# Odd dilated scores: four 64x64 quarters replaced by two 64x128 halves with zero queries

## The chip, the cores and the metric

The kernel runs on one core of a Trainium2 chip. The metric is device time in microseconds (us) for one launch. Before the change it is 736.02 us, the median of three runs from 735.62 to 736.18. One more execution was recorded by the hardware profiler; it took 735.57 us, and its trace spans 733.8 us from the first to the last instruction. The TensorE matmul unit is called PE in the profile and its weight load PEld; VectorE is DVE, ScalarE is ACT, GpSimd is POOL, and SP issues most DMAs.

## The reference, cut to what matters

The network has 256 tokens of width 1024 and two layers. Layer 0 (even) mixes tokens with neighbourhood and latent attention, layer 1 (odd) with dilated sliding windows; each is followed by a squared-ReLU MLP. Only the odd layer's attention is touched. It has three groups of 16 heads, each head 64 wide, with its own queries, keys and values after rotary embedding:

```python
DIL_PAIRS = ((128, 1), (512, 4), (2048, 16))   # (window, dilation)
...
offsets = [jnp.arange(-(w // 2), w // 2 + 1, d) for (w, d) in DIL_PAIRS]
...
kpos = qpos[:, None] + offsets[gi][None, :]
valid = (kpos >= 0) & (kpos < s)
sc = jnp.einsum('bqhd,bqjhd->bhqj', q_blk[:, :, gi], k_sel) * scale
```

Group 0 lets a query see every key within 64 positions. Group 1 lets it see keys whose distance is a multiple of 4, group 2 a multiple of 16; with 256 tokens their windows cut off next to nothing. The three groups are combined by their softmax denominators, which is one softmax over all the scores of a query together.

## The kernel before, in words

**Token order.** The host permutes the tokens so that positions 64c to 64c+63 hold the 64 tokens with the same remainder c modulo 4. A query of group 1 or 2 sees keys of its own class of 64 only. The 256 tokens are two token tiles of 128, and each tile holds two classes. Masks take away what a group does not see.

**Precision.** The projections are computed from f32 numbers split into a high and a low part (lines 178 and 179), with two or three matmuls for each product (lines 182 to 184, 188 and 189); their operands have the type fp32r. The scores of groups 1 and 2 and the products with the values are plain f32 matmuls; each shows in the trace as two weight loads and two matmuls. PE transposes (line 936) show as one of each.

**The odd layer's order.** The heads are taken two at a time, which gives eight units. For a unit, `qk_steps` (line 859) runs twelve projection steps: three weight tiles b (queries and keys of group 0, queries of groups 1 and 2, keys of groups 1 and 2), two halves f and two halves of the contraction. After the last step of a b, `rope` (line 879) applies the rotary embedding by four small DMAs on SP and three operations on DVE. The last DVE operation writes `q12` or `k12` (line 890). Both are tiles of 128 partitions, two heads of 64 rows each, by two groups by 256 tokens. Each is allocated anew for every unit from two rotating buffers (`unit_tiles`, line 816).

After the sixth step of the next unit's projections, a burst is placed in PE's order by hand (`beside` and `burst`, lines 976 to 991): at some units the products with the values (`mix`, lines 953 and 958), then the transposes of the previous unit's first token tile (`turn`, line 936), the group 0 scores (`two_heads`, line 203), the transposes of the second tile, and the scores of groups 1 and 2 (line 914). There are eight bursts; the first has no transposes and the last comes at step 14 of unit 7. After a burst PE goes on with the projections (lines 188 and 189, or 182 to 184 for the values).

**The lines around the change.** For each token tile i, group g, class c and head j, line 914 multiplies 64 rows (the head's width) by 64 queries as the stationary operand and 64 keys as the moving one. The output has 64 partitions and 64 columns. The four combinations of c and j sit on the four quarters of PE's 128x128 array. A bank of PSUM for each (i, j) holds 256 columns of group 0 scores and 2 x 64 columns of the others. DVE then adds the mask and takes the minimum over 384 columns (line 920), ACT takes the exponential (line 922), and DVE and ACT divide by the sum (lines 923 and 924).

**What sets the order.** Every engine runs its own instructions in order. A planner orders them from the program's order and its priorities, and it places semaphores and buffer addresses; `soon()` and `NORM_PRIO` raise the priority of what empties PSUM. A phase's buffers take the addresses of the phase before and wait for them tile by tile (line 1011). POOL runs a few small operations; in the odd layer that is one reciprocal square root (line 258). SP issues the odd layer's tables (line 813) and then its weights, in order.

Of the kernel before, what the change touches and what calls it, by code (L numbers as in the profile page):

```python
# [16 lines left out]
F32 = mybir.dt.float32  # L17
F32R = mybir.dt.float32r
AF = mybir.ActivationFunctionType
ALU = mybir.AluOpType  # L20
# [3 lines left out]
P = 128  # L24
D = 1024
KT = D // P
T = 256
NT = T // P
# [18 lines left out]
def trunk(ctx, tc, a, out):  # L47
    nc = tc.nc
# [8 lines left out]
    def scratch(shape, name):  # L57

        n = int(np.prod(shape))
        v = work.tile([P, 512], F32, tag="scratch", name=name, bufs=12)[:, :n]  # L60
        if len(shape) == 2:
            v = v.rearrange("p (a b) -> p a b", b=shape[1])
        return v
# [8 lines left out]
    def quarter_pair(name):  # L72
        return pair_tile(act, KT // 2, name, 2, "quarter")

    def halves(z):

        return (z[:, 0, :], z[:, 1, :]) if len(z.shape) == 3 else (z[:, :, 0, :], z[:, :, 1, :])

    def bank(tag):
        return ps.tile([P, 512], F32, tag=tag, name=tag)  # L80
# [88 lines left out]
    def weight():  # L169

        j = state["used"]
        prefetch(j + 1, j + 1)
        prefetch(j + LOAD_AHEAD, j + SPLIT_AHEAD)
        state["used"] = j + 1
        return parts.pop(j)[1:]

    def split(hi, lo, src, eng=None):
        a = nc.scalar.copy(hi, src).ins  # L178
        return a, (eng or nc.vector).tensor_tensor(lo, src, hi.bitcast(F32), op=ALU.subtract).ins  # L179
# [6 lines left out]
    def mm2(o, sh, sl, m, first, last):  # L186

        both = lambda: nc.tensor.matmul(o, sh, m.rearrange("p v n -> p (v n)"), start=first, stop=last)  # L188
        low = lambda: nc.tensor.matmul(o[:, 0:T], sl, m[:, 0, :], start=False, stop=False)  # L189
        for step in (low, both) if last else (both, low):  # L190
            step()

    def joined(dst, o):

        nc.scalar.copy(dst, o[:, T:2 * T])  # L195
        nc.vector.tensor_tensor(dst, dst, o[:, 0:T], op=ALU.add)  # L196

    def two_heads(o, qk, ts):

        for n, (a, b) in enumerate(((0, 0), (0, 1), (1, 0))):  # L200
            for j in range(2):
                pb = slice(64 * j, 64 * j + 64)
                nc.tensor.matmul(o[j], qk[pb, 0, a, ts], qk[pb, 1, b, :], start=n == 0, stop=n == 2)  # L203
# [10 lines left out]
    def soon():  # L214

        return tc.high_priority(DRAIN_PRIO)

    def tok(t):
        return slice(t * P, (t + 1) * P)
# [587 lines left out]
    def odd(op, xT, s):  # L807
# [5 lines left out]
            nc.sync.dma_start(dst, a[nm])  # L813
        mixed = [quarter_pair("oa"), quarter_pair("ob")]

        def unit_tiles(u):
            d = {}
            for n, shape, dt in (("q0", [P, 2, 2, T], F32R), ("q12", [P, 2, T], F32), ("k12", [P, 2, T], F32)):
                d[n] = op.tile(shape, dt, tag=n, name=n, bufs=2)
            return d  # L820

        values = {}
# [36 lines left out]
        def qk_steps(d):  # L859


            hold = {}

            def gemm(b, f, half):
                if f == 0 and half == 0:
                    hold["w"], hold["s"] = weight(), scratch([2, T], "qk")
                if half == 0:
                    hold["p"] = bank("acc")
                (wh, wl), s, pq = hold["w"], hold["s"], hold["p"]
                for k in range(4 * half, 4 * half + 4):  # L870
                    ws = slice((f * KT + k) * P, (f * KT + k + 1) * P)
                    mm2(pq, wh[:, ws], wl[:, ws], xT[:, k], k == 0, k == KT - 1)
                if half == 1:
                    with soon():
                        joined(s[:, f], pq)
                if f == 1 and half == 1:
                    rope(b, s)

            def rope(b, s):
                sw, r1 = scratch([2, T], "sw"), scratch([2, T], "r1")  # L880
                for r in range(0, P, 64):
                    nc.sync.dma_start(sw[r:r + 32], s[r + 32:r + 64])
                    nc.sync.dma_start(sw[r + 32:r + 64], s[r:r + 32])
                nc.vector.tensor_tensor(r1, s, cosT.unsqueeze(1).broadcast_to([P, 2, T]), op=ALU.mult)
                nc.vector.tensor_tensor(sw, sw, sinT.unsqueeze(1).broadcast_to([P, 2, T]), op=ALU.mult)
                if b == 0:
                    nc.vector.tensor_tensor(r1, r1, sw, op=ALU.add)
                    split(*halves(d["q0"]), r1)
                else:
                    nc.vector.tensor_tensor(d[("q12", "k12")[b - 1]], r1, sw, op=ALU.add)  # L890

            return [lambda v=(b, f, h): gemm(*v) for b in range(3) for f in range(2) for h in range(2)]

# [9 lines left out]
        def scores(u, d, between):  # L903

            ss = {(i, j): bank("w") for i in range(NT) for j in range(2)}
            for i in range(NT):
                two_heads([ss[i, j][:, 0:T] for j in range(2)], d["q0"], tok(i))
            between()
            for i in range(NT):
                for g in range(2):  # L910
                    for c in range(2):
                        for j in range(2):
                            pb, own = slice(64 * j, 64 * j + 64), slice(i * P + 64 * c, i * P + 64 * c + 64)
                            nc.tensor.matmul(ss[i, j][64 * c:64 * c + 64, T + 64 * g:T + 64 * g + 64], d["q12"][pb, g, own],
                                             d["k12"][pb, g, own], start=True, stop=True)
            for i in range(NT):
                for j in range(2):
                    sn, pp = scratch([384], "sn"), op.tile([P, 384], F32, tag="pp", name="pp", bufs=4)
                    mn, z, rz = (work.tile([P, 1], F32, tag=v, name=v, bufs=4) for v in ("dmn", "dz", "drz"))
                    nc.vector.tensor_tensor_reduce(out=sn, in0=ss[i, j][:, 0:384], in1=mask[:, i, :], op0=ALU.add, op1=ALU.min,  # L920
                                                   scale=-(HD ** -0.5), scalar=3e38, accum_out=mn)
                    nc.scalar.activation(pp, sn, AF.Exp, bias=mn, scale=-1.0, accum_out=z)
                    nc.vector.reciprocal(rz, z)
                    nc.scalar.activation(pp, pp, AF.Copy, scale=rz)
                    probs[u, i, j] = pp
# [16 lines left out]
        def mix(u0, out_tag):  # L942
# [17 lines left out]
            with soon():  # L960
                split(*halves(mixed[u0 // 4][:, u0 % 4:u0 % 4 + 2]), pvo.rearrange("p (u n) -> p u n", u=2))

        units = [unit_tiles(0)]
        d = units[0]
        products, v_out = value_steps(0)
# [17 lines left out]
        def burst(u):  # L983

            def step():
                if u > 1 and u % 2:
                    mix(u - 3, "acc")
                if u > 0:
                    turn(u - 1, 0, "acc")
                scores(u, units[u], lambda: turn(u - 1, 1, "acc") if u > 0 else None)  # L990
            return step

        for u in range(1, 8):
            units.append(unit_tiles(u))
            placed = {5: burst(u - 1)}
            if u == 7:
                placed[13] = burst(7)
            beside(qk_steps(units[u]) + all_values(u), placed)
# [17 lines left out]
    accs, last, scale = phase("mlp0", mlp_between, xT, s)  # L1016
    xT, s = hand_over_tokens(accs, last, 2, scale)
    accs, last = phase("odd", odd, xT, s)
    xT, s = hand_over(accs, last, 3)
    phase("mlp1", finish, xT, s)  # L1020
# [98 lines left out]
```

## Time and profile before

| what | value |
|---|---|
| time, median of three runs | 736.02 us (735.62 to 736.18) |
| time of the profiled execution | 735.57 us |
| its span | 733.8 us |
| PE matmul busy | 723.0 us, 99% |
| PE weight load busy | 626.1 us, 85% |
| DVE busy | 536.9 us, 73% |
| ACT busy | 452.4 us, 62% |
| POOL busy | 5.7 us, 1% |
| line 914: matmul records | 256, 218 ns each (median) |
| line 914: weight loads | 256, 135 ns each (median) |

The busy time of PE is made of matmuls that overlap: their ends are modelled, and the next one starts before the record of the last is over. So a busy PE is no proof that PE is at its peak, and the distance from one start to the next says more than a duration. Shapes are written rows*columns of the array in use, then the moving operand: "64*128 64x256" is 64 rows by 128 stationary columns with 256 moving columns. In the timeline, neighbouring records of one kind are merged into a row with their count; the first number is the start, the second the length from the first start to the last end.

### The profile page before, as it was taken

The page shows a single profiled execution, that of the slowest core. Times are in us where ns is not written, and L with a number is a line of the kernel's source. Part 1 is how long each engine was busy: PE and PEld are TensorE (multiplying, and loading weights), DVE is VectorE, ACT ScalarE, POOL GpSimd, SP SyncE. Part 2 cuts the span into 40 slices and gives each one's busy share as a digit, 9 for nine tenths or more (in the row PEclk, how much of TensorE's full clock was granted, in tenths as well). Part 3 has the DMA queues.
Part 4 walks back from the last instruction along what each step waited for, and adds up shares of the span by engine and source line. Part 5 has one row for each costly group of instructions (what it writes and reads, how often), then busy time and mean ns, then how long its engine had stood idle before and what let it go on. Part 6 is the DMA issues. An engine that isn't in the chain of part 4 may idle for free.

```text
span 733.8 us, 12891 instructions
## 1 busy us (share of the span) xinstructions
PE 723.0 (99%) x5004; PEld 626.1 (85%) x5004; DVE 536.9 (73%) x1078; ACT 452.4 (62%) x1002; POOL 5.7 (1%) x16
## 2 busy tenths in 40 slices
PE   8999999999999999999999999999999999999996
PEld 5899989888888888888888888888998888888885
DVE  6799859756656656889778889778759666665664
ACT  7687857445445446856777667767857445544541
POOL 0100000000000000000000000000000000000000
PEclk9999999999999999999999999999999999999999
DMA  8864423565565554566755665466345556456501
GB/s 288 340 226 153 146 96 125 210 209 180 186 206 182 186 204 158 198 215 209 245 167 178 205 202 202 154 221 200 130 169 206 196 175 225 174 172 209 181 14 57
DMA packets 26989, 135.72 MB, mean 185 GB/s; under 512 B 4400, under 2 KB 7216, under 8 KB 12336
## 3 DMA queue, kind: packets, MB, share of 16 engines
q1 hardware_dynamic: 26640, 134.69, 53.2%
q8 instruction: 39, 0.64, 0.3%
q10 hardware_dynamic: 288, 0.21, 0.1%
q14 instruction: 22, 0.18, 0.1%
HBM read 127.55 MB, written 1.05 MB: 175 GB/s over the span
## 4 chain that ended last, share of the span: by engine, by line
PE 86%; DVE 4%; DMA 3%; ACT 3%; issue 2%; SPq 1%; POOL 0%; POOLq 0%
PE w L188 16%; PE acc L182 13%; PE acc L183 13%; PE acc L184 13%; PE acc L188 12%; PE w L189 8%; PE acc L189 6%; DVE wlo L179 2%; DMA raw<-in_w_c 1%; DMA raw<-in_w_qk 1%; ACT pp L734 1%; DMA bias<-in_rpb 1%; PE w L203 1%; PE acc L936 1%; PE acc L953 1%
## 5 line engine op out<-in xcount | busy, mean ns | idle before, releaser
L179 DVE TENSOR_TENSOR wlo<-raw,whi 128x512 fp32r<-128x512 f32 (+2 forms) x472 | 301.9, 681 | 70.5 <-ACT whi L178 68.8
L178 ACT CAST whi<-raw 128x512 fp32r<-128x512 f32 (+2 forms) x472 | 262.8, 617 | 86.1 <-issue 70.4
L188 PE MATMUL w<-xT,whi 128*128 128x512 f32 x512 | 178.2, 393 | 0.0
L188 PE MATMUL acc<-xT,whi 128*128 128x512 f32 x384 | 133.1, 395 | 0.0
L189 PE MATMUL w<-xT,wlo 128*128 128x256 f32 x512 | 132.8, 280 | 0.0
L188 PEld LDWEIGHTS w<-xT,whi 128*128 128x128 f32 x512 | 93.6, 188 | 17.3
L189 PEld LDWEIGHTS w<-xT,wlo 128*128 128x128 f32 x512 | 96.4, 188 | 5.3
L189 PE MATMUL acc<-xT,wlo 128*128 128x256 f32 x384 | 99.6, 280 | 0.0
L182 PE MATMUL acc<-whi,h 128*128 128x512 f32 x250 | 98.1, 392 | 0.0
L183 PE MATMUL acc<-wlo,h 128*128 128x512 f32 x250 | 97.5, 390 | 0.0
L184 PE MATMUL acc<-whi,h 128*128 128x512 f32 x250 | 97.4, 390 | 0.0
L188 PEld LDWEIGHTS acc<-xT,whi 128*128 128x128 f32 x384 | 69.6, 188 | 12.8
L195 ACT COPY up<-w 128x256 f32<-128x256 f32 x64 | 23.9, 373 | 87.3 <-PE w L188 87.2
L189 PEld LDWEIGHTS acc<-xT,wlo 128*128 128x128 f32 x384 | 72.2, 188 | 3.7
L196 DVE TENSOR_TENSOR up<-up,w 128x256 f32<-128x256 f32 x64 | 26.8, 419 | 61.4 <-ACT up L195 61.4
L184 PEld LDWEIGHTS acc<-whi,h 128*128 128x128 f32 x250 | 46.9, 188 | 9.8
L183 PEld LDWEIGHTS acc<-wlo,h 128*128 128x128 f32 x250 | 47.0, 188 | 9.6
L182 PEld LDWEIGHTS acc<-whi,h 128*128 128x128 f32 x250 | 47.0, 188 | 8.8
L183 PE MATMUL acc<-wlo,xT 128*128 128x512 f32 (+1 forms) x128 | 50.4, 394 | 0.8 <-DVE wlo L179 0.8
L182 PE MATMUL acc<-whi,xT 128*128 128x512 f32 (+1 forms) x128 | 50.5, 394 | 0.5 <-ACT whi L178 0.5
L184 PE MATMUL acc<-whi,xT 128*128 128x512 f32 (+1 forms) x128 | 50.0, 391 | 0.0
L855 ACT ACTIVATE v<-acc,rstd 64x128 f32<-64x128 f32 x64 | 22.8, 362 | 19.7 <-PE acc L184 14.0
(203 smaller groups left out, 981.7 us busy)
## 6 DMA issues: line engine op xcount, KB each, us to landing
raw<-in_w SPq DMA_DIRECT2D x64, 1024.0 KB, 4.8
raw<-in_w_oqk SPq DMA_DIRECT2D x24, 1024.0 KB, 5.0
raw<-in_w_ov SPq DMA_DIRECT2D x12, 1024.0 KB, 5.3
sw<-qk SPq DMA_DIRECT2D x96, 64.0 KB, 3.1
raw<-in_w_qk SPq DMA_DIRECT2D x4, 1024.0 KB, 11.1
raw<-in_w_oe SPq DMA_DIRECT2D x4, 1024.0 KB, 5.0
raw<-in_w_oo SPq DMA_DIRECT2D x4, 1024.0 KB, 5.9
bias<-in_rpb SPq DMA_DIRECT2D x8, 256.0 KB, 4.3
```

Of the source, the lines that this page charges most:

```text
L178: a = nc.scalar.copy(hi, src).ins
L179: return a, (eng or nc.vector).tensor_tensor(lo, src, hi.bitcast(F32), op=ALU.subtract).ins
L182: nc.tensor.matmul(o, sh, mh, start=first, stop=False)
L183: nc.tensor.matmul(o, sh, ml, start=False, stop=False)
L184: nc.tensor.matmul(o, sl, mh, start=False, stop=last)
L188: both = lambda: nc.tensor.matmul(o, sh, m.rearrange("p v n -> p (v n)"), start=first, stop=last)
L189: low = lambda: nc.tensor.matmul(o[:, 0:T], sl, m[:, 0, :], start=False, stop=False)
L195: nc.scalar.copy(dst, o[:, T:2 * T])
L196: nc.vector.tensor_tensor(dst, dst, o[:, 0:T], op=ALU.add)
L203: nc.tensor.matmul(o[j], qk[pb, 0, a, ts], qk[pb, 1, b, :], start=n == 0, stop=n == 2)
L734: nc.scalar.activation(pp[:, j], sn[:, j], AF.Exp, bias=mn[:, j:j + 1], scale=-1.0, accum_out=z[:, j:j + 1])
L855: nc.scalar.activation(v12[64 * g - 64:64 * g, 2 * i + c, :], pq[rows, cs], AF.Copy, scale=ri[rows])
```

## The change

The tile for the queries of groups 1 and 2 is no longer one of two rotating buffers. Two tiles named `spread0` and `spread1` are made once at the start of the odd phase, and the units use them in turn. Each holds, for every group and token tile, three blocks of 64 columns: the queries of class 0, zeros, the queries of class 1. POOL writes the zeros once. The DVE operation at the end of the rotary embedding writes its 512 columns into blocks 0 and 2 instead of into a dense tile.

The scores then take 128 stationary columns: blocks 0 and 1 for class 0 (its queries, then zeros), blocks 1 and 2 for class 1 (zeros, then its queries). The output has all 128 partitions of the bank. The matmul of class 0 starts the accumulation and that of class 1 adds to it in the same 64 columns, so each query's row gets its own class's scores plus zeros. The number of matmuls stays the same (16 in a burst, 128 in all), and so do the moving columns.

```diff
+        spread = [op.tile([P, 2 * NT, 3, 64], F32, name=f"spread{i}") for i in range(2)]
+        for z in spread:
+            nc.gpsimd.memset(z[:, :, 1, :], 0.0)
+
         def unit_tiles(u):
             d = {}
-            for n, shape, dt in (("q0", [P, 2, 2, T], F32R), ("q12", [P, 2, T], F32), ("k12", [P, 2, T], F32)):
+            for n, shape, dt in (("q0", [P, 2, 2, T], F32R), ("k12", [P, 2, T], F32)):
                 d[n] = op.tile(shape, dt, tag=n, name=n, bufs=2)
+            d["q12"] = spread[u % 2]
             return d
...
+                elif b == 1:
+                    own = lambda z: z.rearrange("p g (t c n) -> p (g t) c n", t=NT, c=2)
+                    nc.vector.tensor_tensor(d["q12"][:, :, 0:3:2, :], own(r1), own(sw), op=ALU.add)
                 else:
-                    nc.vector.tensor_tensor(d[("q12", "k12")[b - 1]], r1, sw, op=ALU.add)
+                    nc.vector.tensor_tensor(d["k12"], r1, sw, op=ALU.add)
...
                     for c in range(2):
                         for j in range(2):
                             pb, own = slice(64 * j, 64 * j + 64), slice(i * P + 64 * c, i * P + 64 * c + 64)
-                            nc.tensor.matmul(ss[i, j][64 * c:64 * c + 64, T + 64 * g:T + 64 * g + 64], d["q12"][pb, g, own],
-                                             d["k12"][pb, g, own], start=True, stop=True)
+                            nc.tensor.matmul(ss[i, j][:, T + 64 * g:T + 64 * g + 64], d["q12"][pb, 2 * g + i, c:c + 2, :],
+                                             d["k12"][pb, g, own], start=c == 0, stop=c == 1)
```

## The prediction

> **What bounds the kernel now.** I read the page's share of engines first, then the busy time in the stretches of the odd layer, then PE's timeline around a burst, then the weight loads grouped by shape.
>
> ```profile
> PE 723.0 (99%) x5004; PEld 626.1 (85%) x5004; DVE 536.9 (73%) x1078; ACT 452.4 (62%) x1002; POOL 5.7 (1%) x16
> ...
> 306.00:330.00 24.00, 24.00 (x142) 20.95 (x142) 20.68 (x41) 14.66 (x35) 0.00 (x0) 1.00 0.64 216
> ...
> sum 224.00, PE 224.00 PEld 193.97 DVE 185.47 ACT 163.64 POOL 0.00; mean PE 28.00 PEld 24.25 DVE 23.18 ACT 20.45 POOL 0.00
> ```
>
> The stretch rows give the length, then the busy time of PE, PEld, DVE, ACT and POOL, the granted clock (1.00) and DMA figures; the last row sums eight stretches from 306 to 530 us, which hold all eight bursts. PE is busy in 224.00 of 224.00 us there. DVE has 38.5 us to spare, ACT 60. So a microsecond added to PE's work in this stage finds no pause in which to disappear. One burst, the second, and the first of all:
>
> ```profile
> 359.68 0.41 PE L936 MATMUL acc<-ident,pp 64*128 64x64 f32 x8
> 359.90 0.96 PE L203 MATMUL w<-q 64*128 64x256 f32 x12
> 360.70 0.53 PE L936 MATMUL acc<-ident,pp 64*128 64x64 f32 x12
> 361.16 0.69 PE L914 MATMUL w<-k,q 64*64 64x64 f32 x32
> 361.78 0.50 PE L188 MATMUL acc<-xT,whi 128*128 128x512 f32 x1
> ...
> 329.87 0.97 PE L203 MATMUL w<-q 64*128 64x256 f32 x12
> 330.78 0.69 PE L914 MATMUL w<-k,q 64*64 64x64 f32 x32
> 331.40 0.50 PE L188 MATMUL acc<-xT,whi 128*128 128x512 f32 x1
> ```
>
> ```profile
> L914 PE MATMUL w<-k,q x256: 218/218/267, 330.8 to 516.0; 64*64 64x64 f32 x128
> L936 PE MATMUL acc<-ident,pp x168: 213/222/273, 359.5 to 515.4; 64*128 64x64 f32 x168
> L203 PE MATMUL w<-q x96: 275/280/383, 329.9 to 514.9; 64*128 64x256 f32 x96
> ```
>
> (Durations are shortest, median, longest in ns.) A merged row's last start is its start plus its length less one duration. In the second burst the last transpose (line 936) starts at 360.70 + 0.53 - 0.222 = 361.01, the quarters (line 914) start at 361.16, and the projection goes on at 361.78. **The stretch that the change touches is 361.78 - 361.01 = 0.77 us.** It holds a pause of 0.15 us from a 64*128 shape to the quarters, 32 records in eight steps of four (last start 361.16 + 0.69 - 0.218 = 361.63, so 0.47 us, 0.06 a step), and a pause of 0.15 us to the full array. In the first burst it begins at the last group 0 score, 329.87 + 0.97 - 0.28 = 330.56, and lasts 0.84 us. That the eight are alike is seen in their busy time:
>
> ```profile
> 330.50:331.80 1.30, 0.69 (x32) 0.56 (x32) 1.00 0.56 126
> ...
> sum 10.45, PE 5.56 PEld 4.46; mean PE 0.69 PEld 0.56
> ```
>
> **The change part by part.** *The matmuls.* Their number and moving columns stay. They use 64 rows and all 128 columns, so two run side by side (the two heads) where four did: 32 records become 16 steps of two instead of eight of four. What a step costs hangs on the weight load, which doubles to 128 columns. The loads, grouped by shape (busy us, mean ns of one):
>
> ```profile
> L203 PEld LDWEIGHTS w<-q 64*128 64x128 f32 x96 | 6.2, 187 | 0.3 <-ACT whi L178 0.3
> L936 PEld LDWEIGHTS acc<-ident,pp 64*128 64x128 f32 x168 | 6.7, 138 | 1.2 <-ACT whi L178 0.7 <-issue 0.2
> L914 PEld LDWEIGHTS w<-k,q 64*64 64x64 f32 x256 | 4.5, 134 | 0.6
> L958 PEld LDWEIGHTS acc<-pts,v 128*64 128x64 f32 x96 | 4.4, 138 | 0.0
> L250 PEld LDWEIGHTS w<-mean,squares 128*128 128x128 f32 x16 | 2.4, 190 | 0.3
> L319 PEld LDWEIGHTS w<-ident,down 128*128 128x128 f32 x16 | 1.8, 140 | 0.8 <-ACT down L317 0.6
> ```
>
> Loads of 64 columns take 134 to 138 ns, loads of 128 columns 187 to 190, whether 64 rows (line 203) or 128 (line 250, a plain f32 matmul like ours). The two rows with 128 columns at 138 and 140 are transposes, whose moving operand is the identity. The difference of about 53 ns for 64 columns makes about 107 ns for 128, with a fixed part that overlaps. The distance from load to load confirms it:
>
> ```profile
> 303.97 0.30 PEld L250 LDWEIGHTS w<-mean,squares 128*128 128x128 f32 x2
> ...
> 359.87 0.55 PEld L203 LDWEIGHTS w<-q 64*128 64x128 f32 x8
> ...
> 359.98 0.67 PEld L203 LDWEIGHTS w<-q 64*128 64x128 f32 x10
> ```
>
> Line 250 moves one column (its matmul is 128x1), so its load alone paces it: 0.30 - 0.19 = 0.11 us apart. Line 203 has our shape and loads for two heads side by side: the ten loads from its second pair on are five pairs, (0.67 - 0.187) / 4 = 0.120 us apart, and there 256 columns are moved as well. The new matmul moves far less: the quarters' step of 0.06 us holds their whole move. So the load sets the step, between 0.11 and 0.120. I take 0.117, near line 203, whose shape and pairing it shares.
>
> Pauses. The transposes already use 64*128, so the 0.15 us before the quarters goes. Line 203 after the transposes shows what stands there: the last of the eight transposes starts at 359.68 + 0.41 - 0.222 = 359.87, and line 203's first loads start at 359.87 too, its second pair at 359.98. So I count 16 steps from the last transpose's start to the last score's, the last one from its load to its matmul. The pause after stays: from the wide shape to the full array it is 0.16 us, by the last transposes, 530.71 + 0.72 - 0.222 = 531.21 to 531.37:
>
> ```profile
> 530.71 0.72 PE L936 MATMUL w<-ident,pp 64*128 64x64 f32 x18
> 531.37 0.39 PE L182 MATMUL acc<-oa,whi 128*128 128x256 f32 x1
> ```
>
> So a stretch becomes 16 x 0.117 + 0.15 = 2.02 us. That is 2.02 - 0.77 = 1.25 more in seven bursts and 2.02 - 0.84 = 1.18 in the first: 7 x 1.25 + 1.18 = **9.9 us**. By 0.11 a step it is 7 x 1.14 + 1.07 = 9.1, by 0.120 it is 7 x 1.30 + 1.23 = 10.3.
>
> A rule stands against the slow load. The Trainium skill (TensorEngine Tiling (Array Packing), Restrictions) says that column tiling disables the fast weight load; the quarters are column tiling and the new shape is not. But TensorE: Matmul & The Clock Gate (Weight-path perf modes) of the same skill gives the fast load only to 128 weights that are not FP32. By the first rule alone the new loads would be as quick as the transposes', by the second as slow as line 203's; the load rows side with the second for everything that is not a transpose.
>
> *The DVE write into blocks 0 and 2, and the zeros.* The eight writes keep 512 elements a partition:
>
> ```profile
> L890 DVE TENSOR_TENSOR q<-r,sw x8: 679/682/686, 326.5 to 508.5; 128x512 f32<-128x512 f32 x8
> ...
> 304.63 0.70 POOL L258 TENSOR_TENSOR rstd<-ms,mhalf 128x2 f32<-128x2 f32 x1 [269.04 <-DVE ms L252]
> ...
> L105 POOL MEMSET mean<- 128x128 f32 x1 | 0.2, 206 | 0.0
> ```
>
> No row shows a write in 64-column pieces. If it took half as long again, eight times 0.34 = 2.7 us would go onto DVE, which has 38.5 spare; the bounds for the path are 0 and, with that cover gone, 2.7; I take 0. The two memsets of 256 columns are at most 0.4 us each by the 0.2 of 128 columns; POOL waits 269 us before its only odd operation, so the cover is that pause. Behind them in POOL's queue stands that operation alone. They must come before 304.63; the tiles whose addresses they take are the MLP's, whose matmuls end ahead of the odd layer's first projection. *Buffer waits.* The next write to a spread tile waits for the scores two units before, as the rotating buffers did. The scores of a burst end 1.25 us later; behind line 914 on PE stand the projections, already counted, and DVE's mask step (line 920) starts that much later with the next unit's projections ahead of the transposes that need its result. *Addresses.* The odd phase needs 2 KB a partition more, which shifts later tiles. The queue on which that could matter is SP's:
>
> ```profile
> SPq L813 <- PE acc L184: 7.9, 1, 7.9
> ```
>
> SP already stands 7.9 us at an odd table until the MLP's matmuls free its place, with the odd weights behind it. PE does not pause for that today. Bounds: nothing, to about 3 us if the shift made weights late; I take nothing.
>
> **Sum.** Span 733.8 + 9.9 = 743.7; the profiled execution 735.57 + 9.9 = 745.5. That execution is 0.45 below the median of the runs, which gives 745.9. I forecast 745.7.
>
> **Rivals.** *Quick loads.* The new loads go like the transposes', with which they share rows, columns and moving width. For it speaks the 138 of line 936; against it that only transposes show it. Step (0.53 - 0.222) / 5 = 0.062; stretch 16 x 0.062 + 0.15 = 1.14; 7 x 0.37 + 0.30 = 2.9 more: 738.7.
>
> *Load and move one after the other.* Two matmuls in a row hit the same rows, and the load cannot run under the move. Step 0.11 + 0.06 = 0.17, stretch 2.87, 7 x 2.10 + 2.03 = 16.7 more: 752.5. Against it: line 203 loads the same rows with 128 columns and moves 256 within 0.120. The Trainium skill (TensorE: Matmul & The Clock Gate, Part 3: Packing small matmuls) states this rule, that a weight load overlaps a running matmul only if the row group differs; by this rule line 203 could not be that fast, so the trace speaks against it.
>
> *Steps at issue pace, not slower.* The first pair of line 203 starts only 359.90 - 359.87 = 0.03 us after the transposes. If wide pairs followed each other so, the stretch would be 16 x 0.03 + 0.15 = 0.63 against 0.77, 1.1 to 1.3 us less in all: 734.7. It decides below (0.77 - 0.15) / 16 = 0.039 a step. Against it: every later pair of the same line is 0.120 apart.
>
> *The forecast and late weights or a reordered plan on top.* Up to 3 us more: 746.5 to 749. For it the SP wait; against it that PE has no pause around it today.
>
> **How the numbers follow.** Forecast 0.78, late weights on top 0.07, quick loads 0.09, one after the other 0.03, issue pace 0.02, no visible change for a reason that I don't see 0.01. The forecast's own range is 735.57 + 9.1 = 744.7 to 736.02 + 10.3 = 746.3. With late weights and small shifts of the plan the range is 743.0 to 749.0; it leaves out the quick loads, the serial ones and those not slower, 0.15. A measurement of this kernel tells about 0.2% (1.5 us) from no change. Slower by more: all cases but the last two, 0.97. Issue pace is 1.3 us, hardly beyond the bound: half of its 0.02 counts as faster and half as the same, which gives faster 0.01 and same 0.02.
>
> **What would show it.** In the profile after, the score loads should be 64*128 at about 187 ns; a row of 32 score matmuls should last about 1.8 to 2.0 us instead of 0.69; the pause between the transposes and the scores should be gone and that after them still 0.15. PE should stay busy without a pause from 306 to 540, with the eight stretches carrying nearly all of the growth of the span; DVE's write should stay at 0.68. A load of 138 ns would prove the forecast wrong towards 738.7, and a step near 0.17 towards 752.5. Pauses of PE on DVE or on DMA in the odd layer would mean that I missed a wait.

## The result and the profile after

The changed kernel takes 745.62 us (median of four runs, 744.35 to 746.49) against 736.00 before: a ratio of 1.0129, 95% interval 1.0117 to 1.0141. The growth is 9.6 us; 9.7 was forecast. The profiled execution took 746.49 us and spans 744.7.

The page's share of engines, the first and the summing row of the eight stretches of the odd layer (length, then busy PE, PEld, DVE, ACT, POOL, granted clock, DMA), and the one wait of PE in that layer:

```profile
PE 734.0 (99%) x5004; PEld 637.8 (86%) x5004; DVE 538.0 (72%) x1077; ACT 453.6 (61%) x1003; POOL 6.2 (1%) x18
...
306.00:330.00 24.00, 24.00 (x142) 21.12 (x141) 20.68 (x42) 14.99 (x35) 0.57 (x1) 1.00 0.63 222
...
sum 232.00, PE 231.84 PEld 201.95 DVE 185.47 ACT 163.60 POOL 0.57; mean PE 28.98 PEld 25.24 DVE 23.18 ACT 20.45 POOL 0.07
...
PE acc L944 <- DVE qk L196: 0.2, 1, 0.2
```

PE gained 11.0 us of busy time and PEld 11.7, DVE and ACT about one each. PE is still without a pause in the odd layer but for one wait of 0.2 us on DVE, to which I come back below. The number of matmuls is the same, 5004. The second burst in PE's timeline, and the first (line 922 is the former 914, line 944 the former 936):

```profile
363.22 0.53 PE L944 MATMUL acc<-ident,pp 64*128 64x64 f32 x12
363.59 1.95 PE L922 MATMUL w<-k,spread 64*128 64x64 f32 x32
365.47 0.50 PE L188 MATMUL acc<-xT,whi 128*128 128x512 f32 x1
...
331.11 0.98 PE L203 MATMUL w<-q 64*128 64x256 f32 x12
332.00 2.00 PE L922 MATMUL w<-k,spread 64*128 64x64 f32 x32
333.94 0.50 PE L188 MATMUL acc<-xT,whi 128*128 128x512 f32 x1
```

```profile
L922 PEld LDWEIGHTS w<-k,spread x256: 183/188/195, 332.0 to 526.9; 64*128 64x128 f32 x128
L922 PE MATMUL w<-k,spread x256: 272/272/321, 332.0 to 527.0; 64*128 64x64 f32 x128
L922 PEldq EVENT_SEMAPHORE  x1: 51/51/51, 331.9 to 331.9; - x1
```

The 32 records last 1.95 us instead of 0.69. Their first start is 0.06 us after the last transpose's (363.22 + 0.53 - 0.222 = 363.53), so the pause before them is gone. The last of them starts at 363.59 + 1.95 - 0.272 = 365.27: 15 steps in 1.68 us, **0.112 a step**. The projection follows 0.20 later. The stretch is 365.47 - 363.53 = 1.94 us where it was 0.77 to 0.78. In the first burst it is 333.94 - (331.11 + 0.98 - 0.28) = 2.13 against 0.84, with a semaphore instruction of PE's load queue at 331.9. Seven bursts times 1.16 and one of 1.29 make **9.4 us**.

Where along the trace does the growth stand? POOL's two square roots frame the odd layer and the last MLP. Of before, and of after with the two memsets:

```profile
304.63 0.70 POOL L258 TENSOR_TENSOR rstd<-ms,mhalf 128x2 f32<-128x2 f32 x1 [269.04 <-DVE ms L252]
721.09 0.54 POOL L225 TENSOR_TENSOR rstd<-ss,mhalf 128x1 f32<-128x1 f32 x1 [415.76 <-DVE ss L447]
```

```profile
293.61 0.56 POOL L818 MEMSET spread<- 128x256 f32 x2 [258.33 <-PE acc L184]
305.87 0.70 POOL L258 TENSOR_TENSOR rstd<-ms,mhalf 128x2 f32<-128x2 f32 x1 [11.70 <-DVE ms L252]
732.01 0.54 POOL L225 TENSOR_TENSOR rstd<-ss,mhalf 128x1 f32<-128x1 f32 x1 [425.44 <-DVE ss L447]
```

Between them lie 416.46 us before and 426.14 after: 9.7 us more, 9.4 of them in the bursts. The other 0.3 stand at the fourth burst, ahead of its second transposes. PE's rows there, then two of DVE; in each block before first, then after:

```profile
412.25 0.96 PE L203 MATMUL w<-q 64*128 64x256 f32 x12
413.04 0.55 PE L936 MATMUL acc<-ident,pp 64*128 64x64 f32 x12
...
417.11 0.96 PE L203 MATMUL w<-q 64*128 64x256 f32 x12
418.23 0.59 PE L944 MATMUL acc<-ident,pp 64*128 64x64 f32 x12 [0.17 <-DVE qk L196]
```

```profile
410.23 0.41 DVE L196 TENSOR_TENSOR qk<-qk,acc 128x256 f32<-128x256 f32 x1
411.77 0.68 DVE L890 TENSOR_TENSOR k<-r,sw 128x512 f32<-128x512 f32 x1
...
416.56 0.68 DVE L898 TENSOR_TENSOR k<-r,sw 128x512 f32<-128x512 f32 x1
417.76 0.41 DVE L196 TENSOR_TENSOR qk<-qk,acc 128x256 f32<-128x256 f32 x1
```

The transposes start 0.79 us after the group 0 scores before the change and 1.12 after. They write into `acc`, which the DVE operation of line 196 still has to read, and in the changed kernel's plan that operation stands behind the keys' write where it stood ahead of it. So 0.3 us are a wait for DVE and not the matmuls' own time. That DVE is late because of its new order is read from the rows, not tested.

But the first square root already comes 1.24 us later, ahead of all that was changed. The stretches of after from 80 to 84 us, in the even layer, show a reason:

```profile
80.00:82.00 2.00, 2.00 (x11) 1.87 (x10) 2.00 (x5) 1.08 (x5) 0.00 (x0) 0.57 1.00 422
82.00:84.00 2.00, 2.00 (x13) 2.00 (x12) 1.52 (x6) 1.77 (x8) 0.00 (x0) 0.58 0.26 41
```

The granted clock was 0.57 there, where the kernel before had 1.00. Whether that belongs to the change is the question of the first experiment.

### The profile page after: what moved, and what is told of

It reads as the page before. It is cut to its first block, busy times and chain, and to the rows that moved or that the text cites. A ratio compares the mean times of both kernels' runs of the same rounds, so it can differ in the third digit from the quotient of the medians.

```text
span 744.7 us, 12889 instructions
## 1 busy us (share of the span) xinstructions
PE 734.0 (99%) x5004; PEld 637.8 (86%) x5004; DVE 538.0 (72%) x1077; ACT 453.6 (61%) x1003; POOL 6.2 (1%) x18
## 4 chain that ended last, share of the span: by engine, by line
PE 83%; DVE 6%; ACT 4%; DMA 3%; issue 2%; SPq 1%; POOL 0%; POOLq 0%; DVEq 0%; ACTq 0%
PE w L188 16%; PE acc L182 13%; PE acc L183 12%; PE acc L184 12%; PE acc L188 10%; PE w L189 8%; PE acc L189 5%; DVE wlo L179 3%; PE w L922 2%; DMA sw<-qk 1%; DMA raw<-in_w_v 1%; ACT pp L734 1%; ACT whi L178 1%; PE acc L944 1%; PE w L701 1%
```

## The experiments

**The theory** is the prediction's: a step of the wide form lasts as long as the load of its 128 columns, PE has no slack, and all else costs nothing. **Rivals:** the price is that two matmuls and not four share the array; what is moved or accumulated sets the step; tiles, zeros and the write in pieces cost part of it.

**The changed kernel again.** No edit.

> The changed kernel again, for the interval and for a profile to set the others against. 745.4 within 1. The profile of the change showed a granted clock of 0.57 between 80 and 84 us, in the even layer, and a shift of 1.24 us from there on. Theory (that is this execution's, not the change's): without it the shift up to 300 us is within 0.4 us, and 9.4 to 9.8 us come in the odd layer. Rival (the new layout costs 1.2 us in the even layer): the shift is there again.

Measured: 745.82 us, ratio 1.0144 (1.0122 to 1.0166). The square roots in its trace:

```profile
305.12 0.69 POOL L258 TENSOR_TENSOR rstd<-ms,mhalf 128x2 f32<-128x2 f32 x1 [11.70 <-DVE ms L252]
731.44 0.54 POOL L225 TENSOR_TENSOR rstd<-ss,mhalf 128x1 f32<-128x1 f32 x1 [425.63 <-DVE ss L447]
...
80.00:82.00 2.00, 2.00 (x22) 1.87 (x22) 1.65 (x3) 1.36 (x3) 0.00 (x0) 1.00 0.83 307
```

The clock is 1.00 from 80 to 82 us, the first root comes 0.49 late and the two lie 426.32 apart, 9.9 more than before. But this execution has a stretch of low clock too, at another place:

```profile
8.00:10.00 2.00, 1.88 (x6) 1.74 (x6) 1.66 (x5) 2.00 (x6) 0.00 (x0) 0.50 0.93 300
```

So the place at 80 us was that execution's own. Of the first four runs of the changed kernel two, 744.35 and 745.65 us, have a mean granted clock of 0.999; 3 us at half the clock would take about 0.002 off the mean of a 744 us run (an estimate), so these two had no such stretch and still show the growth. The 0.49 was expected to stay within 0.4; the same row of the next experiment, whose scores alone differ, is 0.8 early, so single executions differ that much:

```profile
303.82 0.70 POOL L258 TENSOR_TENSOR rstd<-ms,mhalf 128x2 f32<-128x2 f32 x1 [11.70 <-DVE ms L252]
```

The 9.9 for the odd layer is a little over the 9.8 expected. PE's wait at the fourth burst is there again, 0.2 us.

**Quarters on the new tiles.**

```diff
-nc.tensor.matmul(ss[i, j][:, T + 64 * g:T + 64 * g + 64], d["q12"][pb, 2 * g + i, c:c + 2, :],
-                 d["k12"][pb, g, own], start=c == 0, stop=c == 1)
+nc.tensor.matmul(ss[i, j][64 * c:64 * c + 64, T + 64 * g:T + 64 * g + 64], d["q12"][pb, 2 * g + i, 2 * c, :],
+                 d["k12"][pb, g, own], start=True, stop=True)
```

> The changed kernel with its tiles, zeros and the write in pieces, but line 914's four 64x64 quarters back (the zeros are then read by nobody). Theory (all of the 9.6 us are the wide matmuls on PE): as before, 736.0 within 0.7, a burst's quarters again 0.48 us from first to last start. Rival (tiles, zeros, the write in pieces or the shifted addresses cost part of it): up to 3 us more, 737.5 to 739.

Measured: 735.87 us, ratio 1.0004 (0.9995 to 1.0014). Its burst:

```profile
360.35 0.69 PE L922 MATMUL w<-k,spread 64*64 64x64 f32 x32
360.97 0.50 PE L188 MATMUL acc<-xT,whi 128*128 128x512 f32 x1
```

The burst is the old one, 0.69. Tiles, zeros, the write in pieces and the shifted addresses cost nothing that can be measured; that rival is out, and the growth comes with the form of the matmuls. PE has no wait in the odd layer here, so the wait and the new order on DVE come with that form too.

**Two quarters at a time.** The kernel before, with the class as the outer loop and the second transposes between the classes.

```diff
-            between()
-            for i in range(NT):
-                for g in range(2):
-                    for c in range(2):
+            for c in range(2):
+                for i in range(NT):
+                    for g in range(2):
                         for j in range(2):
...
+                if c == 0:
+                    between()
```

> The kernel before, with the eight quarter matmuls of class 0 ahead of the second transposes and the eight of class 1 behind them, so that only two quarters have work at a time, as in the wide form, with loads of 64 columns. Theory (the load of 128 columns makes the step): the step stays at 0.059, each group of eight steps lasts 0.46 from first to last start; 0.47 us of steps and about 0.23 of two more pauses are added in seven bursts and at most 0.47 in the first: 741 to 741.5. Rival (the step is long because two matmuls and not four share the array): steps of 0.112, groups of 0.83, 746 to 747.

Measured: 741.42 us, ratio 1.0080 (1.0065 to 1.0095). One burst; its score matmuls last 218 ns each:

```profile
361.22 0.68 PE L913 MATMUL w<-k,q 64*64 64x64 f32 x16
361.83 0.59 PE L937 MATMUL acc<-ident,pp 64*128 64x64 f32 x12
362.35 0.68 PE L913 MATMUL w<-k,q 64*64 64x64 f32 x16
```

A group of eight steps takes 0.68 - 0.218 = 0.46 us from first to last start, as four quarters at a time did (0.69 - 0.218 = 0.47). So a pair of quarters steps as fast as four, and **having only two at a time costs twice the steps but not longer ones**. The 0.83 of the rival is out.

**The move doubled, in the wide form and in the quarters.** The keys go through twice; the second copy lands in columns that are written over or not read. The edit in the changed kernel; in the kernel before it is the same with the quarter's output rows.

```diff
-nc.tensor.matmul(ss[i, j][:, T + 64 * g:T + 64 * g + 64], d["q12"][pb, 2 * g + i, c:c + 2, :],
-                 d["k12"][pb, g, own], start=c == 0, stop=c == 1)
+nc.tensor.matmul(ss[i, j][:, T + 64 * g:T + 64 * g + 128], d["q12"][pb, 2 * g + i, c:c + 2, :],
+                 d["k12"][pb, g, own].unsqueeze(1).broadcast_to([64, 2, 64]), start=c == 0, stop=c == 1)
```

> The changed kernel with each class's 64 keys moved twice (128 moving columns; the second copy goes to columns that are overwritten or not read). Theory (the load sets the step): the move still fits under the load, step 0.112 to 0.12, 745.2 to 746.8. Rival (what is moved or written to PSUM sets the step): 0.17 to 0.22 a step, 753 to 760.

> The kernel before with the same doubling of the keys moved, in the quarters. Theory (in the quarters the load of 64 columns and the move of 64 in two passes are about equal, 0.053 each): the move takes over, step 0.109, 8 x 0.05 more in a burst, 3.2 in all: 739.2. If the move were hidden under the load there as well: 736.0.

Measured: the wide form 747.19 us, ratio 1.0155 (1.0140 to 1.0170); the quarters 739.83, ratio 1.0056 (1.0041 to 1.0071). A burst of the wide form, then one of the quarters with its matmuls' durations:

```profile
362.60 2.00 PE L922 MATMUL w<-k,spread 64*128 64x128 f32 x32
364.53 0.51 PE L188 MATMUL acc<-xT,whi 128*128 128x512 f32 x1
```

```profile
360.74 1.10 PE L914 MATMUL w<-k,q 64*64 64x128 f32 x32
361.77 0.50 PE L188 MATMUL acc<-xT,whi 128*128 128x512 f32 x1
...
L914 PE MATMUL w<-k,q x256: 269/269/320, 330.0 to 520.1; 64*64 64x128 f32 x128
```

In the wide form twice the move costs 0.05 us a burst (2.00 against 1.95), in the quarters 0.41 (1.10 against 0.69): there (1.10 - 0.269) / 7 makes 0.119 a step on average, where it was 0.067. These averages hold a longer first step. The rows of the burst without its first four records, before and with the move doubled:

```profile
361.26 0.59 PE L914 MATMUL w<-k,q 64*64 64x64 f32 x28
...
360.90 0.94 PE L914 MATMUL w<-k,q 64*64 64x128 f32 x28
```

The first step is 361.26 - 361.16 = 0.10 and 360.90 - 360.74 = 0.16; the six others take (0.59 - 0.218) / 6 = 0.06 and (0.94 - 0.269) / 6 = 0.11. So a step that moves 128 columns in the quarters lasts no longer than the wide form's 0.112, and in the wide form such a move lies under the load and does not set the step. The wide kernel's 747.19 is 0.4 above the range expected, the quarters' 739.83 is 0.6 above 739.2. Each has a wait of PE for DVE in the odd layer (the first row is of the wide kernel, the second of the quarters); why DVE is later there was not tested:

```profile
PE w L922 <- DVE k L898: 0.4, 1, 0.4
```

```profile
PE acc L936 <- DVE qk L196: 1.4, 1, 1.4
```

In the quarters the wait is enough for the difference. The wide kernel's profiled execution, with its wait, took 746.58 us and lies in the range; the two of its four runs that lie above, 747.80 and 748.03, have its lowest mean granted clocks, 0.996 and 0.995.

**Fewer columns for class 0.** Class 1 goes first on 128 columns, class 0 second on 96 or 72, written over instead of added. That leaves out the group 1 and 2 scores of 32 or 8 queries in each token tile.

```diff
-                    for c in range(2):
+                    for c in (1, 0):
...
+rows = slice(0, 96 if c == 0 else P)      # 72 in the other kernel
+qs = d["q12"].rearrange("p b c n -> p b (c n)")[pb, 2 * g + i, 64 * c:64 * c + rows.stop]
+nc.tensor.matmul(ss[i, j][rows, T + 64 * g:T + 64 * g + 64], qs,
+                 d["k12"][pb, g, own], start=True, stop=True)
```

> The changed kernel with class 1 first on 128 stationary columns and class 0 second on 96 columns, written over the first instead of added; class 1's queries 0 to 31 of each token tile lose their scores of groups 1 and 2. Theory (step = load of the columns): every second pair loads 96 columns, 0.027 less, 8 x 0.027 = 0.21 less in a burst, 1.7 in all below the changed kernel: 743.7. Rival (the step belongs to the 64*128 shape or to pairs, whatever the columns): as the changed kernel, 745.4.

> As the one with 96 columns, but class 0 on 72 columns (class 1 loses the scores of 8 queries). Theory: those steps go to about 0.065, 8 x 0.047 = 0.38 less in a burst, 3.0 in all: 742.4. Rival: 745.4. If loads go by whole groups of 32 columns, 72 goes like 96.

> The kernel with class 0 on 96 columns once more, since its first profile came from a disturbed execution. Theory: its 96-column steps at 0.085 to 0.09, between 0.112 for 128 columns and 0.065 for 72; 743.7 to 744.5. If loads went by whole groups of 64 columns: 0.112 throughout and 745.4.

Measured: 96 columns 743.47 us, the median of three runs (the profiled execution took 2549 us and is left out), ratio 1.0111 (1.0093 to 1.0130); the same kernel again, for its profile, 743.90, ratio 1.0105 (1.0090 to 1.0120); 72 columns 742.97, ratio 1.0097 (1.0082 to 1.0112). The loads and a burst with 96 columns (from the second time), then with 72:

```profile
L924 PEld LDWEIGHTS w<-k,spread 64*96 64x96 f32 x128 | 8.2, 162 | 0.0
...
361.98 1.74 PE L924 MATMUL w<-k,spread 64*128 64x64 f32 x32
363.65 0.51 PE L188 MATMUL acc<-xT,whi 128*128 128x512 f32 x1
```

```profile
L924 PEld LDWEIGHTS w<-k,spread 64*72 64x72 f32 x128 | 6.9, 141 | 0.0
...
362.38 1.58 PE L924 MATMUL w<-k,spread 64*128 64x64 f32 x32
363.89 0.50 PE L188 MATMUL acc<-xT,whi 128*128 128x512 f32 x1
```

The last matmuls last 0.245 and 0.225 us here. So 15 steps take 1.74 - 0.245 = 1.495 and 1.58 - 0.225 = 1.355; eight of them are still 0.112. The other seven are (1.495 - 0.896) / 7 = 0.086 for 96 columns and (1.355 - 0.896) / 7 = 0.066 for 72. Array form, pairing, move and number of matmuls are the same; only the columns loaded differ, and with them the partitions written, but what is written does not set the step: twice as much of it left the wide form's burst within 0.05 us. **The step follows the columns: 72, 96 and 128 give 0.066, 0.086 and 0.112.** Whole groups of 32 would have put 72 at 96's step; it is not so. The bursts are 8 x (1.95 - 1.74) = 1.7 and 8 x (1.95 - 1.58) = 3.0 us shorter than the changed kernel's, as expected. The times are a coarser measure: against 745.62 to 745.82 they are 1.7 to 2.4 (96 columns, both times) and 2.7 to 2.9 us less, and PE waits 0.9 and 0.8 us for DVE in these two odd layers, where it waited 0.2.

**Heads apart.**

```diff
-                    for c in range(2):
-                        for j in range(2):
+                    for j in range(2):
+                        for c in range(2):
```

> The changed kernel with the head loop outside the class loop: both classes of head 0, then both of head 1, so that neighbours in PE's order use the same 64 rows. Theory (two matmuls run side by side only as neighbours in the order): up to twice the steps, 1.2 to 1.8 us more in a burst, 755 to 760. Rival (each half of the rows works off its own matmuls, some way ahead): no change, 745 to 746.

Measured: 745.54 us, ratio 1.0140 (1.0123 to 1.0157). A burst:

```profile
362.02 2.00 PE L922 MATMUL w<-k,spread 64*128 64x64 f32 x32
363.95 0.50 PE L188 MATMUL acc<-xT,whi 128*128 128x512 f32 x1
```

It is 0.05 us longer than with the heads side by side, not twice as long. My theory of this run fell: matmuls run side by side although PE's order puts those of one half of the rows next to each other. Each half works off its own, at least four records ahead, so that every engine runs its instructions in order, as I wrote above, is too strong for PE. PE's wait at the fourth burst is absent here, which about makes up for the longer bursts.

**The wide form in fp32r.** The spread tiles and `k12` are declared F32R instead of F32, so the scores of groups 1 and 2 are of lower precision.

> The changed kernel with queries and keys of groups 1 and 2 as fp32r, so that each matmul is one load and one pass instead of two; the scores are then of lower precision. Theory (one 128-column load a step, 0.112): eight steps instead of sixteen, a burst 0.9 us shorter than in the changed kernel, 738 to 738.5, still slower than before. Rival (the price hangs on plain f32, not on the columns): a load near 0.138 and steps near 0.06, 734.5 to 735.5.

Measured: 739.10 us, ratio 1.0048 (1.0033 to 1.0064). A burst, and the last one, with its wait:

```profile
361.18 1.06 PE L922 MATMUL w<-k,spread 64*128 64x64 f32 x16
...
517.95 1.08 PE L922 MATMUL w<-k,spread 64*128 64x64 f32 x16 [0.62 <-DVE k L898]
```

Half the records, and (1.06 - 0.273) / 7 = 0.112 again, with a matmul of 273 ns: the price is that of the 128 columns, not of plain f32. The time is 0.6 above the range. The last burst now reaches its keys before DVE has written them and waits 0.62, but the profiled execution, with that wait, took 738.49 us and lies in the range; the two slowest of the six runs, 740.33 and 741.26, have mean granted clocks of 0.996 and 0.995. Why the median lies above stays open. Even with half the loads the wide form is slower than the quarters. No run beat the kernel before.

## Why the prediction was right, step by step

- *PE bounds the odd layer, so added work counts in full.* Right: 9.4 us more in the bursts, 9.7 to 9.9 in the span of the odd layer and what follows.
- *The old step, 0.06.* Right for the regular ones, by a count that was off: eight steps have seven distances, 0.067 on average with the longer first one. The sum used the whole 0.47 and does not suffer.
- *The load of 128 columns sets the step.* Right, shown by three runs: the step follows the columns loaded, not the move, and is not longer with two matmuls side by side than with four. The quick loads of the transposes were not to be had: the new loads take 188 ns.
- *The step, 0.117.* A little too long: 0.112. I leaned to line 203 (0.120), which shares shape and pairing, but it moves 256 columns; the same shape in fp32r with 64 columns moved steps at 0.112 (the last experiment), and line 250, with hardly a move, had the right number (0.11). Too much by 16 x 0.005 x 8 = 0.6 us.
- *The pause before goes.* Right; the first wide pair comes 0.06 after the last transpose, so even less than the step counted, another 0.4 us too much in all.
- *The pause after stays at 0.15.* Wrong by 0.05 in each burst, 0.4 in all: it is 0.20. I took it from the transposes, whose matmuls last 0.222. The rows show the pause to follow the length of the last matmul: 0.20 after 0.272 (wide), 0.18 after 0.245 (96 columns), 0.16 after 0.225 (72), 0.15 after 0.218 (quarters), and 0.20 after 0.269 in the quarters with the move doubled, from 360.74 + 1.10 - 0.269 = 361.57 to 361.77. It is the length less about 0.07 each time. Line 203 with its 0.280 would have been the row to take.
- *The first burst, 1.18 more.* It was 1.29: PE's load queue has a semaphore instruction at 331.9, while the row of line 898 below (the keys' write) ends then too. That this write is what it waits for is read from the two times, not tested.
- *Tiles, zeros and the write in pieces at nothing.* Right: the run with quarters on the new tiles is the old time. The write takes 0.68 us as before; POOL's memsets took 0.31 each, 11.7 us ahead of the square root; SP's wait at the odd table is 7.9 again:

```profile
L896 DVE TENSOR_TENSOR spread<-r,sw x8: 679/683/686, 327.7 to 517.8; 128x512 f32<-128x512 f32 x8
L898 DVE TENSOR_TENSOR k<-r,sw x8: 682/688/694, 331.2 to 524.3; 128x512 f32<-128x512 f32 x8
...
SPq L813 <- PE acc L184: 7.9, 1, 7.9
```

- *No new wait of PE, a reordered plan at nothing.* Wrong by 0.3: PE waits for DVE at the fourth burst, and the planner has given DVE another order. The prediction had a reordered plan as a rival, up to 3 us on top, and named a pause of PE on DVE as the sign of a missed wait; it is one, though small.

- *The other rivals.* Load and move one after the other: out, since doubling the move in the wide form cost 0.05 us a burst. The Trainium skill (TensorE: Matmul & The Clock Gate, Part 3: Packing small matmuls) lets a load overlap a running matmul only in another row group; a step of 0.112 with 128 columns loaded and 128 moved in the same rows speaks against that. Steps at issue pace: only the first pair comes early. Late weights: none.

How the 1.16 us of a usual burst come about can now be told apart: eight more steps of the old 0.06 add 0.48, the wider load adds 16 x (0.112 - 0.06) = 0.83, and the pauses, with the quarters' longer first step, give back about 0.15. The small misses nearly cancel (0.6 and 0.4 too much; 0.4, 0.1 and, outside the bursts, 0.3 to 0.5 too little, most of it the wait at the fourth burst), so a forecast within 0.1 us owes something to luck; its terms were good to 0.4 to 0.6 us.

## What to carry to other kernels

Padding the stationary side with zeros to fill the array is not free: in these runs a small matmul's step was the larger of its load (by the columns) and its move, so doubling the columns at 64 moving ones nearly doubled the step, and giving up column quarters doubled the number of steps on top. Before merging quarters, compare what the change of shape costs, about 0.15 us here, with the steps that are added. When a step is to be priced, look for a row in which the suspected part runs alone; the row with the most similar shape can hide a second limit. And a change on one engine can come with another order on a second one: compare the waits too, here worth 0.3 us.

## What was not expected of the hardware

- The pause at a change of array shape is not one figure: it was the last matmul's recorded length less 0.07 us, from 0.15 to 0.20 in these runs.
- Matmuls on different rows ran side by side even when they stood four records apart in PE's order: the burst took 2.00 us instead of 1.95.
- The load's step was fine in columns, not in groups of 32: 72 columns 0.066 us, 96 columns 0.086.
- In both profiled executions of the changed kernel the granted clock fell for 3 to 4 us, in one at 80 us (0.57), in the other at 8 us (0.50). The first square root came 1.24 and 0.49 us later than before; how much of that is the clock's was not told apart.
